# Second sweep of a hybrid encoder layer: the MLA gate product with x as the stationary operand, turned back in 32x32 blocks

## The chip, the cores and the metric

The kernel runs on one core of a Trainium2 chip. The metric is the device time of one execution in microseconds (us), the median of several runs. The profile is of one further execution; its span is counted from the first to the last instruction that the profiler recorded.

The names of the engines follow the profile: PE is TensorE (its weight loads are PEld), DVE is VectorE, ACT is ScalarE, POOL is GpSimd, and SP is the engine whose queue issues nearly all transfers (DMA).

## What is computed

One layer of an encoder over 2048 tokens of width 1024. An input projection of x feeds two groups of heads: a gated linear attention (GLA) and a multi-head latent attention (MLA). The change concerns the gate of the MLA group alone:

```python
h = x @ w_in                      # m_gate: the last 512 columns
...
def mla_branch(c_q, c_kv, k_rope, gate, ...):
    ...
    o = o.transpose(1, 0, 3, 2, 4).reshape(B, S, D_MLA)
    return o * jax.nn.silu(gate)
...
    return jnp.concatenate([o_a, o_b], axis=-1) @ w_out
x = layer_norm(DEEPNORM_ALPHA * x + mixed, ln_g, ln_b)
```

All matrix products of the projections are made from fp32r operands split into a high and a low part: high x high, high x low and low x high are accumulated, so one product over one block of 128 inputs is three matmuls.

## The kernel before, in words

The kernel has four stretches. Sweep A (0 to about 349 us) goes through the 16 chunks of 128 tokens backwards for the GLA. Sweep C, the second sweep (about 349 to 581 us), goes forward in 8 steps of two chunks each. Then come 16 blocks of softmax attention (to about 1110 us), and last the output projection of the 16 chunks with the layer norm, whose first chunks are mixed into the last attention block.

A step of sweep C (`sweep_c`) does for its two chunks j = 0 and 1: the product `ipm` (`c_ip`, matmuls of 448 columns) for the compressed q and kv, the end of the GLA (`Ob`, `c_oib` to `c_oT`), transposes (`tm`), the rotary q (`pqr`), the absorbed q (`pq`) and the MLA gate (`pz`). Each helper `c_...` is one entry with a place, a number in units of a step (tables `PLACE_C`, `PLACE_C_FIRST`, `PLACE_C_LAST`). All entries are sorted by place, and each engine, SP's queue among them, executes its instructions in that order (`in_order`). So a waiting instruction holds up everything behind it on its engine.

The gate before: `c_pz` multiplies 256 tokens at once. The weights are stationary (one 128x128 block for a head h and an input block k), x of both chunks moves, 256 columns wide: 4 heads x 8 blocks x 3 = 96 matmuls a step, in 8 pieces of 12, into a tile `pz` of two PSUM banks, with channels on partitions and tokens along the free axis. Then `c_gm1` to `c_gm3` on ACT (exp, ln(1 + .), exp) and `c_gm4` on DVE make silu of 128x1024 numbers, and `c_sgm` stores them to the scratch tensor `gm_s`. That layout, channels by tokens, is the one the output projection needs.

Buffers that matter here. PSUM tag `gp` has two slots; `Ob`, `pz` and `pq` rotate through them, so `Ob` of the second chunk waits until `gm4` has read `pz`, and the next step's `pz` waits until `c_og` has read that `Ob`. In SBUF the gate tile has tag `gm` with one buffer, and the low part of the absorbed q (`c_qal`) uses the same tag: `gm1` of a step must wait until the store of the previous step's `qal` (`c_sqa`) has landed. The tile `og` (`c_sqO`) has tag `og` with two buffers. `xch` and `xcl`, the split x of the step, have one buffer; `c_xh` and `c_xl` overwrite one chunk's half for the next step.

In the output projection `OutProj.load` issues for a chunk, on SP in this order: four loads of the GLA output `oa_s` (each fills 32 partitions, in runs of 32 numbers, which completes a transpose that DVE made within blocks of 32x32), one load of the gate from `gm_s`, one of the softmax row factors `r_s` and one of the attention output `ob_s`. `gate` on POOL multiplies the attention output by both, `hi` (ACT) and `lo` (POOL) split the result, `part` multiplies. For chunk c the order of work is: split of chunk c+2, load of chunk c+4, product of c, `finish` of c with its stores.

Of the kernel before, what the change touches and what calls it, by code (L numbers as in the profile page):

```python
# [18 lines left out]
P = 128  # L19
S = 2048  # L20
D = 1024
NK = D // P
NCH = S // P
H = 4
# [5 lines left out]
QB = 512  # L30
NQB = S // QB
# [97 lines left out]
    part=(1.05, 2.03, 5.45, 8.05, 10.24, 17.37, 21.96, 27.24),  # L129
# [3 lines left out]


SETUP_C = ("lset", "u15", "u14", "wS", "wH", "wL", "pb0", "wa0", "wh0", "wl0", "pb1", "wa1", "wh1", "wl1")
STEP_C = ("gm1", "gm2", "gm3", "gm4", "sgm", "pq", "qah", "qal", "sqa")
CHUNK_C = ("lx", "xh", "xl", "lS", "lq", "lo", "lu", "sqm", "ssm", "rml", "rmd", "cq", "ckv", "krf", "krfa",
    "krsh", "krsl", "vh", "vl", "kvx", "tm", "cqTh", "cqTl", "ckvTh", "ckvTl", "krT", "pqr", "qrf", "qrfa",
    "tq", "qrTh", "qrTl", "Sf1", "Sf2", "M", "Ob", "oib", "sqO",
    "ss", "rgl", "rgd", "og", "oT", "soT")  # L140

FETCH_C = ("lx", "xh", "xl")
LAST_C = ("ckvTh", "ckvTl", "krT")
# [14 lines left out]
    xh=(-0.19, -0.054),  # L158
    sqO=(0.272, 0.94),
    rgl=(0.283, 1.029),  # L160
# [10 lines left out]
    oT=(0.392, 1.103),  # L171
    oib=(0.24, 0.881),
    ss=(0.278, 1.005),
    rgd=(0.359, 1.067),
# [20 lines left out]
    lx=(-0.578, -0.186),  # L195
    soT=(1.119, 1.45),
    pz=(0.25, 0.306, 0.318, 0.429, 0.527, 0.531, 0.557, 0.559),
    gm1=0.823,
    gm2=0.832,
    gm3=0.837,  # L200
    gm4=0.845,
    sgm=1.17,
    pq=1.435,
    qah=1.501,
# [66 lines left out]
    lx=(-3.463, 0.129),  # L271
    soT=(1.342, 1.45),
    pz=(-0.249, -0.195, -0.111, -0.018, 0.405, 0.452, 0.485, 0.622),
    gm1=0.643,
    gm2=0.815,
    gm3=0.82,
    gm4=0.83,
    sgm=1.056,
    pq=1.431,
    qah=1.57,  # L280
# [50 lines left out]
    lx=(-0.48, -0.573),  # L331
    soT=(1.29, 2.304),
    pz=(0.572, 0.578, 0.707, 0.845, 0.918, 1.023, 1.1, 1.22),
    gm1=1.309,
    gm2=1.608,
    gm3=1.859,
    gm4=1.953,
    sgm=2.042,
    pq=1.525,
    qah=1.948,  # L340
# [13 lines left out]
class K:  # L354
# [151 lines left out]
    def run(self):  # L506
        tc, nc, ins = self.tc, self.nc, self.ins
        with ExitStack() as top:
            cp = top.enter_context(tc.tile_pool(name="const", bufs=1))
            self.cp = cp  # L510
            dp = top.enter_context(tc.tile_pool(name="scr", bufs=1, space=DRAM))
            self.qd_s = [dp.tile([P, H * P], F32, name=f"qd_s{c}") for c in range(NCH)]
            self.oi_s = [dp.tile([P, H * P], F32, name=f"oi_s{c}") for c in range(NCH)]
            self.su_s = [dp.tile([P, H * P], F32, name=f"su_s{c}") for c in range(NCH)]
            self.u_s = [dp.tile([P, H * P], F32, name=f"u_s{c}") for c in range(NCH)]
            self.qa_s = [[dp.tile([P, H, QB], F32, name=f"q{p}_s{b}") for p in "hl"] for b in range(NQB)]
            self.qr_s = [dp.tile([2, QB // P, P, 256], F32, name=f"qr_s{b}") for b in range(NQB)]
            self.gm_s = [dp.tile([P, H, QB], F32, name=f"gm_s{b}") for b in range(NQB)]
            self.kv_s = dp.tile([NCH, 3, P, P], F32, name="kv_s")
            self.oa_s = [dp.tile([H, P, P], F32, name=f"oa_s{c}") for c in range(NCH)]  # L520
            self.qk_s = [[dp.tile([64, H, P], F32, name=f"{n}_s{c}") for c in range(NCH)] for n in ("qx", "kx")]
            self.kt_s = [dp.tile([P, H, P], F32, name=f"kt_s{c}") for c in range(NCH)]
            self.r_s = [dp.tile([1, H, QB], F32, name=f"r_s{b}") for b in range(NQB)]
            self.ob_s = [dp.tile([P, H, QB], F32, name=f"ob_s{b}") for b in range(NQB)]

            ident = cp.tile([P, P], F32, name="ident")
            self.ident = ident
            self.gkv_c = cp.tile([P, 1], F32, name="gkv_c")
            self.gn_c = cp.tile([P, 1], F32, name="gn_c")
# [24 lines left out]
            self.ckvT_h, self.ckvT_l, self.kr = (self.kvT[:, :, i] for i in range(3))  # L554
            self.vh = rp.tile([P, NKT, P], F32R, name="vh")
            self.vl = rp.tile([P, NKT, P], F32R, name="vl")
            self.sweep_c()
            bcs.close()
            psum.close()
            self.wof = top.enter_context(tc.tile_pool(name="wof", bufs=PRE_W, side="right", reuse_waits="tile"))  # L560
            self.attention()
# [693 lines left out]


    def c_pz(self, s, n):
        last = s["st"] == NCH // 2 - 1
        if n == 0:
            s["pz"] = self.gp.tile([P, H, 256], F32, tag="gp", name=f"pz{s['st']}")  # L1260
        order = [(h, k) for h in range(H) for k in range(NK)]
        if last:
            order = [(h, k) for p in range(2) for k in range(NK) for h in (p, p + 2)]
        x2 = lambda t, k: t[:, k].rearrange("p a t -> p (a t)")
        part = [(h, k, p) for h, k in order[4 * n:4 * n + 4] for p in range(3)]
        if n == 0 and s["st"]:

            part.sort(key=lambda e: e[2] == 1)
        stop = {h: (k, p) for h, k, p in part if k == NK - 1}
        for h, k, p in part:  # L1270
            w, x = ((0, self.xch), (0, self.xcl), (1, self.xch))[p]
            self.nc.tensor.matmul(s["pz"][:, h], self.Wz[k][w][:, h * P:(h + 1) * P], x2(x, k),  # L1272
                                  start=(k == 0 and p == 0), stop=stop.get(h) == (k, p))

    def c_gm1(self, s):
        s["gm"] = self.w1.tile([P, H, 256], F32, tag="gm", name=f"gm{s['st']}")
        self.nc.scalar.activation(s["gm"], s["pz"], AF.Exp, scale=-1.0)

    def c_gm2(self, s):
        self.nc.scalar.activation(s["gm"], s["gm"], AF.Ln, bias=1.0)  # L1280

    def c_gm3(self, s):
        self.nc.scalar.activation(s["gm"], s["gm"], AF.Exp, scale=-1.0)

    def c_gm4(self, s):
        self.nc.vector.tensor_tensor(s["gm"], s["pz"], s["gm"], ALU.mult)

    def of_step(self, s):
        return s["st"] // 2, slice((s["st"] % 2) * 256, (s["st"] % 2) * 256 + 256)

    def c_sgm(self, s):
        b, qs = self.of_step(s)
        self.nc.sync.dma_start(self.gm_s[b][:, :, qs], s["gm"])

    def c_pq(self, s):
        pq = s["pq"] = self.gp.tile([P, H, 256], F32, tag="gp", name=f"pq{s['st']}")
# [8 lines left out]
        self.hi(s["qh"], s["pq"])  # L1305

    def c_qal(self, s):
        s["ql"] = self.w1.tile([P, H, 256], F32R, tag="gm", name=f"qal{s['st']}")
        self.lo(s["ql"], s["pq"], s["qh"])

    def c_sqa(self, s):
        b, qs = self.of_step(s)
        for t, dst in zip((s["qh"], s["ql"]), self.qa_s[b]):
            self.nc.sync.dma_start(dst[:, :, qs], t.bitcast(F32))

    def c_sqr(self, s, j):
        b, qs = self.of_step(s)
# [586 lines left out]
class OutProj:  # L1904
# [39 lines left out]
    def load(self, o):  # L1944
# [7 lines left out]
        else:  # L1952
            gr = self.gr[c % 2] = self.gr.get(c % 2) or self.slot(f"gr{c}").rearrange("p a (b d) -> p a b d", b=4)
        o["gr"] = gr
        for r, src in kern.blocks_of(kern.oa_s[c].rearrange("h p (m t) -> h p m t", t=32)):
            nc.sync.dma_start(of[r, 0].rearrange("p h (b t) -> p (h b) t", t=32), src)
        nc.sync.dma_start(gr[:, 0], kern.gm_s[b][:, :, cs])
        nc.sync.dma_start(gr[:, 1], kern.r_s[b][:, :, cs].to_broadcast([P, 4, P]))
        nc.sync.dma_start(of[:, 1], kern.ob_s[b][:, :, cs])
        o["oh"], o["ol"] = [], []  # L1960
# [158 lines left out]
```

## Time and profile before

| | |
|---|---|
| median of 3 runs | 1261.82 us (1261.12 to 1262.24) |
| the profiled execution's own time | 1264.79 us |
| its span | 1262.9 us |
| PE busy | 1239.1 us, 6848 matmuls |
| DVE, ACT, POOL busy | 896.3, 729.1, 726.5 us |
| granted TensorE clock, mean | 0.997 of full speed |
| moved by DMA | 165.59 MB in 277393 packets, 178630 of them under 512 B |

A row of the timeline has the start in us, the duration, the engine, the source line, the operation, its tiles as out<-in and, in brackets, the idle time of the engine before it with what ended it. Matmuls are pipelined: one shows a duration of 0.28 us and more although the next starts 0.12 us later, so the cost of a matmul is read from the distance of starts. Rows of a table of stretches give busy time and instruction count for each engine, then the granted clock, the busy share of the 16 DMA engines and GB/s.

### The profile page before, as it was taken

To read this page: it belongs to the slowest core of one execution; us is meant where nothing else is said; L and a number is where in the kernel's file an instruction comes from. 1 tells how busy PE (TensorE), PEld (TensorE's weight loads), DVE (VectorE), ACT (ScalarE), POOL (GpSimd) and SP (SyncE) were. 2 spreads that over 40 slices of the span, in tenths; PEclk is the share of its full clock that TensorE was granted. 3 is DMA by queue.
4 is the path that set the end of the run, shared out by engine and by line. 5 is a ranking of instruction groups with operands and counts; after the bars stand their busy time and mean duration, and the time that the engine had idled before them with its cause. 6 is when DMAs were issued, how large, how long until landed. Compare 5 with 4: busy or idle time off the path is not lost.

```text
span 1262.9 us, 19554 instructions
## 1 busy us (share of the span) xinstructions
PE 1239.1 (98%) x6848; PEld 1089.6 (86%) x6848; DVE 896.3 (71%) x1666; ACT 729.1 (58%) x1149; POOL 726.5 (58%) x443
## 2 busy tenths in 40 slices
PE   7999999999999999999999999999999999999997
PEld 7999999999899999988788888888888888887886
DVE  6635454554565666665899999999999998378767
ACT  6643434444564444544888888888888888411210
POOL 0132323232355556530798888889999999935551
PEclk9999999999999999999999999999999999999999
DMA  8225555555757788868412222202234110487773
GB/s 294 68 84 130 134 143 139 144 139 144 266 180 212 212 247 244 245 184 210 79 28 49 43 50 43 53 15 59 59 93 93 41 42 26 125 206 212 198 210 100
DMA packets 277393, 165.59 MB, mean 131 GB/s; under 512 B 178630, under 2 KB 234830, under 8 KB 277296
## 3 DMA queue, kind: packets, MB, share of 16 engines
q1 hardware_dynamic: 276176, 162.23, 48.3%
q0 software_dynamic: 672, 2.10, 0.4%
q8 instruction: 54, 0.88, 0.3%
q14 instruction: 43, 0.35, 0.1%
q10 hardware_dynamic: 448, 0.03, 0.0%
HBM read 105.54 MB, written 58.75 MB: 130 GB/s over the span
## 4 chain that ended last, share of the span: by engine, by line
PE 84%; DVE 4%; DMA 4%; POOL 2%; issue 2%; ACT 2%; SPq 1%; DVEq 0%; POOLq 0%; ACTq 0%
PE pz L1272 7%; PE ipm L1341 5%; PE pS L1605 5%; PE pS L1607 4%; PE pS L1606 4%; PE pS L1608 4%; PE pS L1609 4%; PE o L421 4%; PE o L419 4%; PE o L420 4%; PE ipa L419 4%; PE ipa L421 4%; PE ipa L420 4%; PE ipg L421 2%; PE ipg L419 2%
## 5 line engine op out<-in xcount | busy, mean ns | idle before, releaser
L371 POOL TENSOR_TENSOR pl<-s,ph 128x1024 fp32r<-128x1024 f32 x128 | 306.8, 2416 | 47.2 <-ACT ph L365 37.0
L1614 ACT ACTIVATE s<-pS 128x1024 f32<-128x1024 f32 x128 | 131.5, 1028 | 52.9 <-PE pS L1609 49.0
L1627 DVE TENSOR_TENSOR rm<-pS,rm 128x512 f32<-128x512 f32 x210 | 144.6, 689 | 18.3 <-ACT s L1614 12.7
L1651 DVE TENSOR_TENSOR s<-s,mb 128x1024 f32<-128x1024 f32 x128 | 151.2, 1213 | 9.0 <-PE mb L1645 8.9
L365 ACT ACTIVATE ph<-s 128x1024 fp32r<-128x1024 f32 x128 | 134.8, 1056 | 15.7 <-PE o L421 15.1
L1655 ACT ACTIVATE s<-s 128x1024 f32<-128x1024 f32 x128 | 131.6, 1051 | 10.3 <-DVE s L1651 9.6
L419 PE MATMUL ipa<-wah,xah 128*128 128x384 f32 (+1 forms) x384 | 129.2, 336 | 6.1 <-ACT wah L365 6.1
L420 PE MATMUL ipa<-wal,xah 128*128 128x384 f32 (+1 forms) x384 | 125.0, 325 | 0.0
L421 PE MATMUL ipa<-wah,xal 128*128 128x384 f32 (+1 forms) x384 | 124.7, 325 | 0.0
L1091 POOL TENSOR_TENSOR Sb<-Sb,Us 64x512 f32<-64x512 f32 x15 | 19.9, 1327 | 171.5 <-DVE Us L1083 162.3
L1605 PE MATMUL pS<-qh,kvT 128*128 128x512 f32 x256 | 102.6, 401 | 0.8 <-DVE rm L1627 0.4
L419 PE MATMUL o<-ph,vh 128*128 128x512 f32 x256 | 100.9, 394 | 0.0
L1607 PE MATMUL pS<-qh,kvT 128*128 128x512 f32 x256 | 100.0, 391 | 0.0
L1606 PE MATMUL pS<-ql,kvT 128*128 128x512 f32 x256 | 100.0, 390 | 0.0
L421 PE MATMUL o<-ph,vl 128*128 128x512 f32 x256 | 99.8, 390 | 0.0
L1608 PE MATMUL pS<-rh,kvT 128*128 128x512 f32 x256 | 99.8, 390 | 0.0
L1609 PE MATMUL pS<-rl,kvT 128*128 128x512 f32 x256 | 99.8, 390 | 0.0
L420 PE MATMUL o<-pl,vh 128*128 128x512 f32 x256 | 99.7, 389 | 0.0
L1678 DVE TENSOR_TENSOR ap<-ap,s 128x512 f32<-128x512 f32 x120 | 82.9, 691 | 2.7 <-ACT s L1655 0.7
L419 PEld LDWEIGHTS ipa<-wah,xah 128*128 128x128 f32 x384 | 73.3, 191 | 9.3 <-ACT wah L365 6.4
L371 POOL TENSOR_TENSOR ol<-of,oh 128x512 fp32r<-128x512 f32 x32 | 42.5, 1328 | 59.8 <-ACT oh L365 47.4
L1272 PE MATMUL pz<-xch,wzh 128*128 128x256 f32 x256 | 73.4, 290 | 1.4 <-DVE og L1529 1.3
(308 smaller groups left out, 3404.9 us busy)
## 6 DMA issues: line engine op xcount, KB each, us to landing
xcf<-xT_dram SPq DMA_DIRECT2D x16, 512.0 KB, 5.5
xr<-x_dram SPq DMA_DIRECT2D x16, 512.0 KB, 6.0
out_dram<-rr SPq DMA_DIRECT2D x32, 256.0 KB, 3.5
xaf<-xT_dram SPq DMA_DIRECT2D x14, 512.0 KB, 4.2
oib<-oi_s SPq DMA_DIRECT2D x16, 256.0 KB, 4.9
qdb<-qd_s SPq DMA_DIRECT2D x16, 256.0 KB, 3.5
SU<-su_s SPq DMA_DIRECT2D x16, 256.0 KB, 5.0
ub<-u_s SPq DMA_DIRECT2D x16, 256.0 KB, 4.1
```

What stands on the lines that cost most here:

```text
L371: return e.tensor_tensor(dst, src, hi.bitcast(F32), ALU.subtract).ins
L419: mm(out, ah, bh, start=start, stop=False)
L420: mm(out, ah, bl, start=False, stop=False)
L421: mm(out, al, bh, start=False, stop=stop)
L1272: self.nc.tensor.matmul(s["pz"][:, h], self.Wz[k][w][:, h * P:(h + 1) * P], x2(x, k), start=(k == 0 and p == 0), stop=stop.get(h) == (k, p))
L1605: mm(ps[:, e], kh, qh, start=True, stop=False)
L1606: mm(ps[:, e], kh, ql, start=False, stop=False)
L1607: mm(ps[:, e], kl, qh, start=False, stop=False)
L1608: mm(ps[:, e], kr, rh, start=False, stop=False)
L1609: mm(ps[:, e], kr, rl, start=False, stop=True)
L1627: V.tensor_tensor(d["rm"], src[:, e], d["rm"], ALU.max)
L1651: V.tensor_tensor(s, s, d["mb"][:, None, :].to_broadcast([P, 2, QB]), ALU.subtract)
```

## The change

The product is turned round. x of one chunk is stationary, and 512 columns of weights move, so a piece of `pz` is two input blocks of one chunk: 6 matmuls of 512 columns. Pieces 0 to 3 belong to chunk 0, pieces 4 to 7 to chunk 1; their places stay. The result has tokens on partitions. The silu is made for each chunk alone (128x512), its last multiplication is written back into PSUM, and a new entry `gmx` turns it in blocks of 32x32 on DVE into SBUF. The scratch tensor becomes `gm_s[step][chunk, head, 128, 128]`, and the output projection completes the transpose on loading, by four loads with runs of 32 numbers instead of one. The low part of the absorbed q leaves the tag `gm`: it is split into two tiles of tag `og`, made by two instructions and stored by two transfers.

```diff
-STEP_C = ("gm1", "gm2", "gm3", "gm4", "sgm", "pq", "qah", "qal", "sqa")
+STEP_C = ("sgm", "pq", "qah", "qal", "sqa")
@@ CHUNK_C
-    "ss", "rgl", "rgd", "og", "oT", "soT")
+    "ss", "rgl", "rgd", "og", "oT", "soT", "gm1", "gm2", "gm3", "gm4", "gmx")
@@ PLACE_C
-    gm1=0.823,
-    gm2=0.832,
-    gm3=0.837,
-    gm4=0.845,
+    gm1=(0.45, 0.823),
+    gm2=(0.46, 0.826),
+    gm3=(0.47, 0.829),
+    gm4=(0.5, 0.832),
+    gmx=(0.76, 0.835),
...
@@ PLACE_C_FIRST
+    gm1=(0.53, 0.643),
+    gm2=(0.55, 0.815),
+    gm3=(0.56, 0.82),
+    gm4=(0.61, 0.83),
+    gmx=(0.81, 0.835),
...
@@ PLACE_C_LAST
+    gm1=(0.9, 1.309),
+    gm2=(0.91, 1.608),
+    gm3=(1.2, 1.859),
+    gm4=(1.26, 1.953),
+    gmx=(1.265, 1.954),
...
-            self.gm_s = [dp.tile([P, H, QB], F32, name=f"gm_s{b}") for b in range(NQB)]
+            self.gm_s = [dp.tile([2, H, P, P], F32, name=f"gm_s{s}") for s in range(NCH // 2)]
...
     def c_pz(self, s, n):
-            s["pz"] = self.gp.tile([P, H, 256], F32, tag="gp", name=f"pz{s['st']}")
...
+            s["pz"] = self.gp.tile([P, 2, 512], F32, tag="gp", name=f"pz{s['st']}")
+        j, half = divmod(n, 4)
+        for k in (2 * half, 2 * half + 1):
+            xh, xl = self.xch[:, k, j], self.xcl[:, k, j]
+            self.mm3(s["pz"][:, j], xh, xl, self.Wz[k][0], self.Wz[k][1], start=(k == 0), stop=(k == NK - 1))
+
+    def gm(self, d):
+        s, j = d["step"], d["j"]
+        if "gm" not in s:
+            s["gm"] = self.w1.tile([P, 2, 512], F32, tag="gm", name=f"gm{s['st']}")
+        return s["gm"][:, j], s["pz"][:, j]
...
+    def c_gm4(self, d):
+        gm, pz = self.gm(d)
+        self.nc.vector.tensor_tensor(pz, pz, gm, ALU.mult)
+
+    def c_gmx(self, d):
+        self.nc.vector.transpose(*self.gm(d))
...
     def c_sgm(self, s):
-        self.nc.sync.dma_start(self.gm_s[b][:, :, qs], s["gm"])
+        self.nc.sync.dma_start(self.gm_s[s["st"]].rearrange("j h p f -> p (j h) f"),
+                               s["gm"].rearrange("p j (h f) -> p (j h) f", h=H))
...
     def c_qal(self, s):
-        s["ql"] = self.w1.tile([P, H, 256], F32R, tag="gm", name=f"qal{s['st']}")
-        self.lo(s["ql"], s["pq"], s["qh"])
+        s["ql"] = []
+        for n in range(2):
+            hs = slice(2 * n, 2 * n + 2)
+            s["ql"].append(self.w1.tile([P, 2, 256], F32R, tag="og", name=f"qal{s['st']}_{n}", bufs=2))
+            self.lo(s["ql"][n], s["pq"][:, hs], s["qh"][:, hs])
...
     def c_sqa(self, s):
+        qh, ql = self.qa_s[b]
+        self.nc.sync.dma_start(qh[:, :, qs], s["qh"].bitcast(F32))
+        for n, t in enumerate(s["ql"]):
+            self.nc.sync.dma_start(ql[:, 2 * n:2 * n + 2, qs], t.bitcast(F32))
...
@@ OutProj.load
-        for r, src in kern.blocks_of(kern.oa_s[c].rearrange("h p (m t) -> h p m t", t=32)):
-            nc.sync.dma_start(of[r, 0].rearrange("p h (b t) -> p (h b) t", t=32), src)
-        nc.sync.dma_start(gr[:, 0], kern.gm_s[b][:, :, cs])
+        for dst, scr in ((of, kern.oa_s[c]), (gr, kern.gm_s[c // 2][c % 2])):
+            for r, src in kern.blocks_of(scr.rearrange("h p (m t) -> h p m t", t=32)):
+                nc.sync.dma_start(dst[r, 0].rearrange("p h (b t) -> p (h b) t", t=32), src)
```

The functions that the new code calls are unchanged: `blocks_of` yields for m = 0 to 3 the 32 partitions from 32m and the source view, and `mm3` issues high x high, high x low, low x high.

More of the change, by code (lines that the diff above doesn't have):

```diff
@@ L273 @@
     pz=(-0.249, -0.195, -0.111, -0.018, 0.405, 0.452, 0.485, 0.622),
[L274 to L277, printed above, removed]
+    gm1=(0.53, 0.643),
[3 more added lines that the diff above has]
+    gmx=(0.81, 0.835),
     sgm=1.056,
@@ L333 @@
     pz=(0.572, 0.578, 0.707, 0.845, 0.918, 1.023, 1.1, 1.22),
[L334 to L337, printed above, removed]
+    gm1=(0.9, 1.309),
[3 more added lines that the diff above has]
+    gmx=(1.265, 1.954),
     sgm=2.042,
@@ L1257, in c_pz @@
     def c_pz(self, s, n):
-        last = s["st"] == NCH // 2 - 1
         if n == 0:
-            s["pz"] = self.gp.tile([P, H, 256], F32, tag="gp", name=f"pz{s['st']}")
[L1261 to L1286, printed above, removed]
+            s["pz"] = self.gp.tile([P, 2, 512], F32, tag="gp", name=f"pz{s['st']}")
[3 more added lines that the diff above has]
+            self.mm3(s["pz"][:, j], xh, xl, self.Wz[k][0], self.Wz[k][1], start=(k == 0), stop=(k == NK - 1))
@@ new lines, in gm, with c_gm1, c_gm2, c_gm3 @@
+    def gm(self, d):
[3 more added lines that the diff above has]
+        return s["gm"][:, j], s["pz"][:, j]
+    def c_gm1(self, d):
+        gm, pz = self.gm(d)
+        self.nc.scalar.activation(gm, pz, AF.Exp, scale=-1.0)
+    def c_gm2(self, d):
+        gm, _ = self.gm(d)
+        self.nc.scalar.activation(gm, gm, AF.Ln, bias=1.0)
+    def c_gm3(self, d):
+        gm, _ = self.gm(d)
+        self.nc.scalar.activation(gm, gm, AF.Exp, scale=-1.0)
@@ L1288, in of_step @@
+    def c_gm4(self, d):
+        gm, pz = self.gm(d)
+        self.nc.vector.tensor_tensor(pz, pz, gm, ALU.mult)
+    def c_gmx(self, d):
+        self.nc.vector.transpose(*self.gm(d))
     def of_step(self, s):
@@ L1291, in c_sgm @@
     def c_sgm(self, s):
-        b, qs = self.of_step(s)
-        self.nc.sync.dma_start(self.gm_s[b][:, :, qs], s["gm"])
+        self.nc.sync.dma_start(self.gm_s[s["st"]].rearrange("j h p f -> p (j h) f"),
+                               s["gm"].rearrange("p j (h f) -> p (j h) f", h=H))
     def c_pq(self, s):
@@ L1307, in c_qal @@
     def c_qal(self, s):
-        s["ql"] = self.w1.tile([P, H, 256], F32R, tag="gm", name=f"qal{s['st']}")
-        self.lo(s["ql"], s["pq"], s["qh"])
+        s["ql"] = []
[3 more added lines that the diff above has]
+            self.lo(s["ql"][n], s["pq"][:, hs], s["qh"][:, hs])
     def c_sqa(self, s):
         b, qs = self.of_step(s)
-        for t, dst in zip((s["qh"], s["ql"]), self.qa_s[b]):
-            self.nc.sync.dma_start(dst[:, :, qs], t.bitcast(F32))
+        qh, ql = self.qa_s[b]
+        self.nc.sync.dma_start(qh[:, :, qs], s["qh"].bitcast(F32))
+        for n, t in enumerate(s["ql"]):
+            self.nc.sync.dma_start(ql[:, 2 * n:2 * n + 2, qs], t.bitcast(F32))
     def c_sqr(self, s, j):
```

## The prediction

> **What bounds the kernel now.** I read the page first (engines, chain), then the waits, the chain and the timeline of sweep C, and last the stretch in which the output projection starts.
>
> ```profile
> span 1262.9 us, 19554 instructions
> PE 1239.1 (98%) x6848; PEld 1089.6 (86%) x6848; DVE 896.3 (71%) x1666; ACT 729.1 (58%) x1149; POOL 726.5 (58%) x443
> GB/s 294 68 84 130 134 143 139 144 139 144 266 180 212 212 247 244 245 184 210 79 28 49 43 50 43 53 15 59 59 93 93 41 42 26 125 206 212 198 210 100
> DMA  8225555555757788868412222202234110487773
> PE 84%; DVE 4%; DMA 4%; POOL 2%; issue 2%; ACT 2%; SPq 1%; DVEq 0%; POOLq 0%; ACTq 0%
> PE pz L1272 7%; PE ipm L1341 5%; PE pS L1605 5%; PE pS L1607 4%; PE pS L1606 4%; PE pS L1608 4%; PE pS L1609 4%; PE o L421 4%; PE o L419 4%; PE o L420 4%; PE ipa L419 4%; PE ipa L421 4%; PE ipa L420 4%; PE ipg L421 2%; PE ipg L419 2%
> ```
>
> PE is the bound, and the gate product heads the chain by line. A shorter `pz` shortens the run unless PE then waits. DMA is busy in sweep C and once more from 1100 us on; both places count below.
>
> In sweep C steps repeat; these are pieces of the chain of work that ended last (start, duration):
>
> ```profile
> 393.90 2.87 PE pz L1272 x24
> 402.33 0.91 PE Ob L1506 x8
> 411.11 6.07 PE pz L1272 x36
> 425.24 2.87 PE pz L1272 x24
> 440.53 4.31 PE pz L1272 x36
> 452.90 2.87 PE pz L1272 x24
> ```
>
> From 425.24 on the last pieces of a step come every 27.66 us (452.90 - 425.24), with PE busy throughout. From 393.90 to 425.24 it is 31.34 us: 3.68 us are lost once, between step 1 and step 2. The timeline shows where:
>
> ```profile
> 393.15 0.52 SPq L1314 DMA_DIRECT2D ql_s<-qal  x1
> 400.31 1.03 ACT L1277 ACTIVATE gm<-pz 128x1024 f32<-128x1024 f32 x1 [2.46 <-DMA qr_s<-qrT]
> 403.55 1.22 DVE L1286 TENSOR_TENSOR gm<-pz,gm 128x1024 f32<-128x1024 f32 x1 [8.78 <-ACT gm L1283]
> 409.80 0.44 PE L1413 MATMUL tm<-ident,cq 128*128 128x128 f32 x2 [0.83 <-ACT cq L1364]
> 411.11 0.39 PE L1272 MATMUL pz<-xch,wzh 128*128 128x256 f32 x1 [0.88 <-DVE og L1529]
> 410.00:416.00 6.00, 5.12 (x30) 4.89 (x29) 5.84 (x22) 3.16 (x14) 4.91 (x6) 0.72 0.82 227
> ```
>
> `gm1` waits for a store although it reads only PSUM: its buffer is the one that `qal` used, and the store issued at 393.15 is not released before 400.3 (the row names `qr_s`, issued behind it; only `ql_s` holds this buffer). So `gm4` starts at 403.55, the DVE queue behind it is late, `tm` and `pz` wait, and the granted clock falls to 0.72: 36 matmuls take 6.07 instead of 4.31 us.
>
> *The skill on this.* The Trainium skill, "TensorE: Matmul & The Clock Gate", Part 1, lets the clock fall after an idle window of about 3.4 us. By it the two waits would be too short and only some 2 us of the 3.68 would belong to this stall, and the sum below would be -1.8. The trace does not agree: the clock fell after two waits of about 1 us.
>
> **The change, part by part.**
>
> *The matmuls.* Price of 512 columns, from the gate product of sweep A, which has this very form (first and last of 18 matmuls in a row):
>
> ```profile
> 344.73 0.39 PE L419 MATMUL ipg<-wgh,xbh 128*128 128x512 f32 x1
> 348.58 0.39 PE L421 MATMUL ipg<-wgh,xbl 128*128 128x512 f32 x1
> ```
>
> (348.58 - 344.73) / 17 = 0.2265 us. Of 256 columns: 4.31 / 36 = 0.1197. A step goes from 96 x 0.1197 = 11.49 to 48 x 0.2265 = 10.87: 0.62 less, 8 steps: -4.9 us. Twice the columns cost nearly twice the time; this is no halving. In the steady steps PE waits for nothing, so it counts in full; bounds: -5.0, and -4.0 if the first and the last step, whose order waits on DVE, keep theirs. I take -4.8.
>
> *The gate tile unshared.* `gm1` now waits only for its own predecessor's store, a step old. `gm4` of step 1 then follows the end of `pz`, about 3 us earlier. The next thing late would be `og`, whose end at 411.1 lets `pz` start; 3 us earlier it ends before `tm`, which then does not wait either. The stall and the clock loss go: -3.7, between 0 (the wait returns elsewhere, below) and -3.7.
>
> *The silu, turning and splitting.*
>
> ```profile
> L1286 DVE TENSOR_TENSOR gm<-pz,gm x8: 1223/1224/1226, 373.5 to 580.5; 128x1024 f32<-128x1024 f32 x8
> L1563 DVE TENSOR_TENSOR gs<-ipg,gs 128x512 f32<-128x512 f32 x14 | 9.7, 690 | 27.4 <-ACT gs L1561 27.4
> L1535 DVE STREAM_TRANSPOSE oT<-og 128x512 f32<-128x512 f32 x16 | 11.4, 711 | 0.5
> L1557 ACT ACTIVATE gs<-ipg 128x512 f32<-128x512 f32 x14 | 8.4, 598 | 40.3 <-PE ipg L421 38.1 <-DMA k<-kx_s 2.2
> 450.90 1.22 DVE L371 TENSOR_TENSOR qal<-pq,qah 128x1024 fp32r<-128x1024 f32 x1 [1.30 <-ACT qah L365]
> 460.01 1.22 DVE L1286 TENSOR_TENSOR gm<-pz,gm 128x1024 f32<-128x1024 f32 x1 [6.23 <-ACT gm L1283]
> 449.84 1.02 ACT L365 ACTIVATE qah<-pq 128x1024 fp32r<-128x1024 f32 x1 [5.08 <-PE pq L421]
> 455.81 1.06 ACT L365 ACTIVATE xch<-xcf 128x1024 fp32r<-128x1024 f32 x1 [2.28 <-PE pz L1272]
> ```
>
> DVE: one 1.22 becomes 2 x (0.69 + 0.71) = 2.80 a step, and `qal` 1.22 becomes 1.38: +1.7 us. ACT: each 128x1024 becomes two of about 0.6, so +0.5 us. Chunk 0's silu needs `pz` only up to piece 3, which ends before `pq`; three ACT operations (1.9 us) fit in the 5.08 idle before `qah`, `gm4` in the 1.30 before `qal`, `gmx` in the 6.23 after it. Chunk 1's chain after the last piece becomes 3 x 0.6 + 1.4 = 3.2 instead of 4.3, and `xch` of chunk 0 need no longer wait 2.28 for the second half of `pz`. So everything that was tight behind `gm4` (the bank for `Ob`) gets 1 to 3 us of room. Cost on the path: 0; if the cover ahead of `qal` failed, the 0.69 of `gm4` would hold up `qal` and the bank that it frees, 8 times: 5.5.
>
> *SP and stores in sweep C.* One more issue a step (0.52, the row at 393.15), and the gate's store in runs of 512 B instead of 1 KB.
>
> ```profile
> 427.01 0.42 SPq L1318 DMA_DIRECT2D qr_s<-qrT  x1
> 434.60 0.32 SPq L1467 DMA_DIRECT2D qdb<-qd_s  x1
> ```
>
> These two follow each other in SP's queue, so it stands idle for 7 us in a step; 0. The second `og` of a step now waits for the first stored half of `qal`. In step 1 that store was released at 400.3, and `og` comes after `Ob`, which ends at 403.2: some 3 us of room.
>
> *The loads of the output projection.* This is the price. Each chunk trades one load of 512 packets of 512 B for four with 2048 packets of 128 B, three more issues.
>
> ```profile
> 720.00:730.00 10.00, 10.00 (x50) 8.28 (x49) 8.49 (x11) 7.08 (x8) 8.16 (x4) 1.00 0.82 131
> 750.00:760.00 10.00, 10.00 (x49) 8.29 (x48) 8.44 (x12) 7.13 (x8) 8.19 (x5) 1.00 0.62 131
> 1108.00:1128.00 20.00, 20.00 (x92) 16.57 (x91) 14.28 (x29) 2.49 (x7) 7.71 (x6) 1.00 0.92 205
> 1170.00:1230.00 60.00, 60.00 (x267) 49.66 (x266) 42.07 (x71) 9.32 (x23) 34.94 (x24) 1.00 0.73 208
> 1128.30 2.73 SPq L2048 DMA_DIRECT2D out_dram<-rr  x4
> 1135.35 1.29 DVE L2032 SCALAR_TENSOR_TENSOR rr<-xr,po 128x512 f32<-128x512 f32 x2 [1.78 <-DMA out_dram<-rr]
> 1139.59 0.63 ACT L365 ACTIVATE oh<-of 128x512 fp32r<-128x512 f32 x1
> 1147.03 0.50 PE L421 MATMUL pmb<-woh,ol 128*128 128x512 f32 x1 [1.00 <-POOL ol L371]
> 1218.39 1.92 SPq L1956 DMA_DIRECT2D of<-oa_s  x4
> 1234.19 2.98 POOL L1965 TENSOR_TENSOR of<-of,gr 128x512 f32<-128x512 f32 x2
> ```
>
> The first two rows hold one query fetch of attention each: 4096 packets of 128 B and 384 of 2 KB. 0.62 x 10 us x 16 engines = 99 engine-us. At 23 GB/s an engine (294 / (0.8 x 16), first slice) the 384 take 34, which leaves 16 ns a small packet; all on the small ones is 24, the busier fetch (131) at most 32. I take 20. The load then costs 2048 x 0.020 - 512 x 0.022 = 30 engine-us more, 1.9 us of all 16 engines a chunk (1.4 to 3.4).
>
> Three such loads, of chunks 4 to 6, are issued in the 20 us before the stores at 1128.30, where DMA is 0.92 busy and leaves 1.6 us free. Behind them in SP's queue stand the x loads and the stores at 1128.30, whose landing frees the buffer for the residual at 1135.35; `finish`, in front of chunk 6's split on ACT (1139.59), follows it, and PE already waits for that split at 1147.03. There is no slack, so 3 x 1.9 = 5.6, less 1.6, arrives on PE: 4.0 to 5.6, and 0.5 for the later wait behind the next x load: +5.0 (1.0 if only the issues count, 3 x 0.48 less the room; more in the second rival).
>
> Later it is hidden: chunk 15's load starts at 1218.39 and the gate takes it at 1234.19. Of these 15.8 us some 4 go to the issues and up to 7 to the landing (the slow store at 393.15); the 5 left cover the 1.9 and three issues of 0.48 (1.92 / 4). 127 of 174 engine-us a chunk (0.73 x 16 x 10.9 us) become 157.
>
> *The skill on this.* The Trainium skill, "DMA: Bandwidth & Descriptors", Specifications, asks for at least 512 B a transfer and says that smaller ones are read, modified and written. As an estimate, 128 B would then cost no less than 512 B, 22 ns, the load 34 engine-us, and the tail about 0.8 us more than by the 20 that the fetch shows: -2.7 for the sum below, inside the forecast's own range.
>
> *Sum.* -4.8 - 3.7 + 5.0 = -3.5. The profiled execution, 1264.79 (span 1262.9 and 1.9 around it), becomes 1261.3; the median lies 2.97 below that execution, so 1258.3.
>
> **The rivals.**
>
> *The tail absorbs the loads.* If small packets cost 16 ns and the 0.08 free share takes most of it, PE loses 1.0: -7.5, 1254.3. For it: from 1170 on a quarter of DMA is free. Against: the chain through 1135.35 has no room.
>
> *The tail chokes (slower).* One mechanism: the queue of 128 B packets between 1107 and 1140. At 32 ns a chunk costs 3.4 us more; four chunks (4 to 7) 13.6, less 2.7 free: 10.9, and the wait of PE at chunk 6 becomes long enough for the clock, 1.8 as at 411.11: 12.7 in place of 5.0, so +4.2, 1266.0. It decides from (174 - 127 + 11) / 2048 = 28 ns, where the steady chunks fill DMA too. For it: the busier fetch. Against: most fetches show 0.62.
>
> *The stall only moves.* `og`, waiting for `qal`'s store, keeps ACT's queue late in step 1: -4.8 + 5.0 = +0.2, 1262.0. For it: DMA is saturated there, and a store took 7 us. Against: the 3 us of room computed above.
>
> **How the numbers follow.** Forecast 0.42 (own range 1256.3 to 1260.3, the tail between 3 and 7), absorbed 0.20, choked 0.20, moved 0.18. A measurement can tell 0.2%, 2.5 us, from no change: faster is below 1259.3, slower above 1264.3 or, for a case near zero with its own scatter, a part of it. Faster: two thirds of the forecast (0.28) and absorbed (0.20), 0.48. Same: a third of the forecast (0.14) and two thirds of moved (0.12), 0.26. Slower: choked (0.20) and the rest of moved (0.06), 0.26. The range reaches below the absorbed case, where its 1.0 can vanish, and to the choked one: 1253.0 to 1266.0.
>
> **What would show it.** Starts of `pz` matmuls 0.2265 apart and steps of about 27.0 us; no DMA wait ahead of `gm1`, step 1 to 2 as long as the others, clock 1.00 at 410; DMA share above 0.95 between 1108 and 1140, PE's wait for chunk 6 about 4 us longer, no new wait after 1170. I am wrong if `pz` starts waiting for `gm4` or `gmx`, or if chunks after 7 wait for their loads.

## The result, and the profile after

| | before | after |
|---|---|---|
| median of six runs, us | 1261.6 (1260.62 to 1262.24) | 1272.28 (1269.66 to 1273.28) |
| ratio, 95% interval | | 1.0082 (1.0069 to 1.0095) |
| the profiled execution, its span | 1264.79, 1262.9 | 1272.72, 1271.0 |

The changed kernel is 10.7 us slower. The prediction said 1258.3, with 1253.0 to 1266.0 as the range.

The page of the changed kernel (span, engines, DMA packets, and engines along the chain that ended last):

```profile
span 1271.0 us, 18931 instructions
PE 1239.7 (98%) x6464; PEld 1070.6 (84%) x6464; DVE 909.3 (72%) x1698; ACT 733.3 (58%) x1173; POOL 726.0 (57%) x443
DMA packets 306960, 165.56 MB, mean 130 GB/s; under 512 B 212294, under 2 KB 264398, under 8 KB 306864
PE 81%; issue 5%; DMA 4%; POOL 3%; DVE 3%; SPq 2%; ACT 2%; DVEq 0%; POOLq 0%; ACTq 0%
```

384 matmuls fewer, and PE is as busy as before: 1239.7 against 1239.1. A busy PE includes matmuls at a lower clock, so the shorter product must have been paid for somewhere. PE's share of the chain fell from 84 to 81%. The list of what PE waited for (total, times, longest) names the places:

```profile
PE ipa L422 <- ACT wah L368: 5.5, 1, 5.5
PE pmb L422 <- DVE rr L2043: 3.5, 3, 1.7
PE pz L422 <- DVE rg_t L446: 2.9, 1, 2.9
PE pqr L424 <- DVE cqT_l L374: 2.2, 1, 2.2
```

The first is the start of the kernel, which the change does not touch. `pmb` (the output projection) waiting for `rr`, and `pz` (the new product) waiting for L446, are new. First the stall that was to go, the same stretch as in the prediction:

```profile
410.00:416.00 6.00, 6.00 (x35) 5.23 (x34) 5.81 (x23) 3.39 (x13) 2.64 (x4) 1.00 0.92 245
```

The clock is 1.00 where it was 0.72: the stall between step 1 and step 2 is gone. But step 0 has a new one. The chain through it, piece by piece (start, duration):

```profile
365.78 0.60 ACT gm L1276
...
366.65 0.53 ACT gm L1280
...
367.20 0.64 ACT gm L1284
...
367.86 0.10 DVE pz L1288
367.96 0.51 issue
368.47 0.16 DVE rg_t L446
368.63 0.78 PE pz L422
369.41 0.43 PE pz L423
369.83 0.43 PE pz L424
```

PE stops after piece 3 and starts piece 4 only when `gm4` of chunk 0 (L1288, issued 367.86, 0.70 long) has ended at 368.56. The chain names `rg_t`, the next instruction on DVE, since it ended nearest; the dependence is on `gm4`. Piece 4 writes `pz[:, 1]`, `gm4` writes `pz[:, 0]`; they share no number, but they are one tile. And after the wait the clock is half: 0.43 us a matmul instead of 0.23, and a granted clock of 0.50 from 369.41 to 371.50.

In the steady steps the same dependence leaves a gap (`gm4` of chunk 0, the last row of `pq` and the first rows of piece 4, then one whole step as a stretch):

```profile
447.22 0.67 DVE L1288 TENSOR_TENSOR pz<-pz,gm 128x512 f32<-128x512 f32 x1
447.65 0.28 PE L424 MATMUL pq<-cqT_h,wabs_l 128*128 128x256 f32 x1
447.94 0.50 PE L422 MATMUL pz<-wzh,xch 128*128 128x512 f32 x1
448.28 0.40 PE L423 MATMUL pz<-wzl,xch 128*128 128x512 f32 x1
```

```profile
426.48:453.93 27.45, 27.44 (x154) 24.49 (x153) 19.42 (x66) 14.44 (x39) 15.13 (x17) 1.00 0.84 240
```

0.29 instead of 0.12 us behind `pq`, 0.34 instead of 0.23 behind the first matmul: a step takes 27.45, not 27.0. In the last step a mere reading does the same: `gm1` of chunk 0 stands right ahead of piece 4 there (places 0.9 and 0.918), and piece 4 waits until `gm1` has read its half:

```profile
570.28 0.60 ACT L1276 ACTIVATE gm<-pz 128x512 f32<-128x512 f32 x1 [1.78 <-PE pz L424]
570.93 0.50 PE L422 MATMUL pz<-wzh,xch 128*128 128x512 f32 x1 [0.69 <-ACT gm L1276]
```

In all sweep C gained nothing and took 1.8 us more: the first score product of attention (`pS`) starts at 580.48, before at 580.50, although the changed execution had entered sweep C 1.8 us earlier (first `ipm` of the sweep at 346.99 against 348.81).

The rest is lost in the output projection. SP's queue, DVE and PE around chunk 4, then the stretches ahead of and behind the stall, after and (counted from the same product, `sx`) before:

```profile
1109.93 2.47 SPq L1968 DMA_DIRECT2D gr<-gm_s  x4
...
1113.60 1.05 SPq L1989 DMA_DIRECT2D xr<-x_dram  x2
...
1121.03 0.27 PE L1758 MATMUL rt<-ident,rc 128*4 128x128 f32 x1 [0.78 <-DVE rc L1746]
...
1122.22 0.69 DVE L2043 SCALAR_TENSOR_TENSOR rr<-xr,pmb 128x512 f32<-128x512 f32 x1 [1.03 <-DMA xr<-x_dram]
...
1123.05 0.77 PE L422 MATMUL pmb<-woh,oh 128*128 128x512 f32 x1 [1.75 <-DVE rr L2043]
...
1133.26 2.54 SPq L2059 DMA_DIRECT2D out_dram<-rr  x4
```

```profile
1107.65:1119.65 12.00, 12.00 (x54) 9.88 (x53) 6.91 (x14) 0.63 (x1) 2.09 (x2) 1.00 0.90 216
1119.65:1129.65 10.00, 7.47 (x29) 5.78 (x28) 8.27 (x19) 1.85 (x6) 4.30 (x4) 0.83 0.64 125
```
```profile
1107.75:1119.75 12.00, 12.00 (x55) 9.88 (x53) 7.77 (x16) 0.63 (x1) 3.46 (x3) 1.00 0.99 229
1119.75:1129.75 10.00, 10.00 (x48) 8.34 (x47) 8.51 (x18) 1.85 (x6) 5.92 (x5) 1.00 0.80 163
```

`pmb` of chunk 4 needs a PSUM bank, which chunk 2's residual (`rr<-xr,pmb`) frees, which waits for its x load, issued at 1113.60 behind the four gate loads. The stores stand in SP's queue 4.96 us later than before (1133.26 against 1128.30). The DMA engines are not what became the limit: their share is 0.90 and then 0.64, in the kernel before 0.99 and 0.80. From the start of attention to chunk 15's product it is 671.25 us (580.48 to 1251.73), before 663.24 (580.50 to 1243.74): 8.0 more.

### The profile page after: what moved, and what is told of

It is laid out like the page before. It is cut to its first block, busy times and chain, and to the rows that moved or that the text cites. A ratio compares the mean times of both kernels' runs of the same rounds, so it can differ in the third digit from the quotient of the medians.

```text
span 1271.0 us, 18931 instructions
## 1 busy us (share of the span) xinstructions
PE 1239.7 (98%) x6464; PEld 1070.6 (84%) x6464; DVE 909.3 (72%) x1698; ACT 733.3 (58%) x1173; POOL 726.0 (57%) x443
## 4 chain that ended last, share of the span: by engine, by line
PE 81%; issue 5%; DMA 4%; POOL 3%; DVE 3%; SPq 2%; ACT 2%; DVEq 0%; POOLq 0%; ACTq 0%
PE ipm L1352 5%; PE o L422 5%; PE o L423 5%; PE o L424 5%; PE pS L1616 4%; PE pS L1618 4%; PE pS L1617 4%; PE pS L1620 4%; PE pS L1619 4%; PE ipa L422 4%; PE ipa L424 4%; PE ipa L423 4%; PE pz L422 2%; PE pz L424 2%; PE pz L423 2%
## 5 line engine op out<-in xcount | busy, mean ns | idle before, releaser
L423 PEld LDWEIGHTS ipa<-wal,xah 128*128 128x128 f32 x384 | 73.0, 190 | 0.8 <-DVE wal L374 0.3
```

Of the source, the lines that this page charges most:

```text
L423: mm(out, ah, bl, start=False, stop=False)
```

## The experiments

Each ratio is to the kernel before, with its 95% interval. The theories after the comparison: the tail pays for the loads (for their packets, or for their number); sweep C pays for the one tile `pz`; or sweep C's end eats any lead.

**The unshared tile alone.** The kernel before, with the `qal` and `sqa` of the change:

```diff
-        s["ql"] = self.w1.tile([P, H, 256], F32R, tag="gm", ...)
+            s["ql"].append(self.w1.tile([P, 2, 256], F32R, tag="og", ..., bufs=2))
```

> The kernel before with one part of the change alone: the low part of the absorbed q in two tiles of tag og, stored by two transfers; product, silu, scratch layout and output projection as before. Both theories expect the stall between step 1 and step 2 (3.68 us) to go, so that the steps from step 2 on start about 3.7 us earlier than before. Theory A (a lead that sweep C gains is kept): attention starts 3.7 us earlier, 1261.6 - 3.7 = 1257.9. Theory B (the last step of sweep C waits for loads that come no earlier, and eats any lead): attention starts at 580.5 as before, 1261.6.

Measured: 1259.26 (0.9987, 0.9978 to 0.9995), 2.5 less. The stretch between step 1 and step 2 is a normal step now:

```profile
394.58:422.24 27.66, 27.66 (x202) 26.97 (x201) 17.90 (x63) 13.85 (x36) 15.13 (x16) 1.00 0.82 242
```

Attention starts at 574.80, 5.7 earlier: 2.0 of this it had already when sweep C began (346.78), 3.7 is the stall. The lead is kept; theory B falls. That the median gained 2.5 and not 3.7 fits the scatter that the last run below shows.

**One gate load; four gate loads with long runs.** The changed kernel with other loads in the output projection:

```diff
-        for dst, scr in ((of, kern.oa_s[c]), (gr, kern.gm_s[c // 2][c % 2])):
...
+        nc.sync.dma_start(gr[:, 0], kern.gm_s[c // 2][c % 2].rearrange("h p f -> p h f"))
```
```diff
+        for m in range(4):
+            r = slice(32 * m, 32 * m + 32)
+            nc.sync.dma_start(gr[r, 0], kern.gm_s[c // 2][c % 2][:, r].rearrange("h p f -> p h f"))
```

> The changed kernel with one gate load per chunk in the output projection again, 512 packets of 512 B; the transpose of the gate that the four loads complete is left out, so the gate factors stand in the wrong places. Theory A (the four loads with 128 B runs cost the tail its 8.0 us): the product of chunk 4 starts at about 1120.1 instead of 1123.05, chunk 15 some 8 us earlier, 1272.3 - 8 = 1264.3. Theory B (the tail lost time to something else that came with the change, the order of its instructions or the clock): less than 3 us back, over 1269.

> The changed kernel with four gate loads per chunk, each of 32 partitions in runs of 512 B: three more issues than the kernel before, its number and size of packets; the transpose of the gate is left out. Theory A (the packets cost): as with one load, about 1264.3. Theory B (the three issues on SP cost, 3 x 0.48 us a chunk ahead of the x loads): most of the 8 us stays, 1269 to 1272.

Measured: 1261.43 (0.9999, 0.9989 to 1.0008) and 1267.14 (1.0049, 1.0034 to 1.0065). So the loads cost 10.8 us, by the medians the whole loss: 5.7 for three more issues a chunk (each of 32 partitions instead of one of 128), 5.1 for runs of 128 instead of 512 B. Neither theory had it alone. How the time gets to PE is seen at chunk 6: the issue of its x load on SP, and its residual on DVE, whose end frees the bank for chunk 8. Before, one load, four long, and the changed kernel:

```profile
1158.56 0.62 SPq L1978 DMA_DIRECT2D xr<-x_dram  x1
1165.21 0.69 DVE L2032 SCALAR_TENSOR_TENSOR rr<-xr,pmb 128x512 f32<-128x512 f32 x1 [5.49 <-DMA xr<-x_dram]
```
```profile
1156.01 0.61 SPq L1989 DMA_DIRECT2D xr<-x_dram  x1
1162.67 0.69 DVE L2043 SCALAR_TENSOR_TENSOR rr<-xr,pmb 128x512 f32<-128x512 f32 x1 [4.87 <-DMA xr<-x_dram]
```
```profile
1159.96 0.62 SPq L1991 DMA_DIRECT2D xr<-x_dram  x1
1166.24 0.69 DVE L2045 SCALAR_TENSOR_TENSOR rr<-xr,pmb 128x512 f32<-128x512 f32 x1 [7.31 <-DMA xr<-x_dram]
```
```profile
1165.93 0.62 SPq L1989 DMA_DIRECT2D xr<-x_dram  x1
1172.24 0.69 DVE L2043 SCALAR_TENSOR_TENSOR rr<-xr,pmb 128x512 f32<-128x512 f32 x1 [7.55 <-DMA xr<-x_dram]
```

In all four the residual follows the issue by 6.3 to 6.7 us. By these rows the load takes no longer with small packets around it; it is issued later. Counted from `sx` (a product for the softmax sums of the last head; 1119.75, 1118.84, 1118.51, 1119.65), the issue comes after 38.8, 37.2, 41.5 and 46.3 us. Part of that is SP's own time for the issues: the gate loads of chunks 4 to 6 take 6.1 us of the queue before (1.44, 3.68 and 0.97) and 9.9 after (2.47, 5.06 and 2.41). Part is a loop that the changed kernel's chain shows from 1109 on (a load's landing, the split on ACT and POOL that frees a buffer, SP's next loads, their landing):

```profile
1109.33 3.68 DMA of<-oa_s
1113.03 0.64 ACT oh L368
1113.74 1.30 POOL ol L374
...
1116.19 2.18 SPq L1968
1118.42 6.01 DMA of<-oa_s
```

The Trainium skill, "Perfetto Trace Analysis", What "DMA-bound" means, tells two main cases apart: the 16 engines, or the sequencer that issues, whose track is then solid. The trace agrees that this is the second: from chunk 4's load to the first stores (1107.90 to 1133.26) the changed kernel's SP has no gap of 0.2 us and waits for a semaphore in 4.8 of the 25.4 us, while the DMA share is 0.64 to 0.90. What made one issue last 2.18 us there, where others take 0.49, stays open.

**The order of the instructions.** With four loads the compiler had also moved two things of the last heads forward: `rt`, which turns softmax row factors, ahead of chunk 4's product on PE, and `rc`, which computes such factors, ahead of chunk 2's residual on DVE. Put back, with four long loads:

```diff
+                            with self.in_order({ENGINES[2]: rest[2]["aggr"]}, ENGINES[2:3]):
+                                f(nb - 1)
...
+                        with self.in_order({ENGINES[0]: pe5}, ENGINES[:1]):
                             turn(nb - 2)
```

> The four gate loads of 512 B runs once more (transpose of the gate left out), with the instructions of TensorE and VectorE in the order of the kernel with one load: rt of the last head but one goes back behind the product of chunk 5, and the sum rc of the last head behind the aggregate of chunk 2. Both had moved forward when the loads became four. Theory A (the three issues on SP, in front of the x loads, cost the 5.7 us between one load and four): 1267. Theory B (the order that the compiler chose costs it: rt and rc stand ahead of pmb): 1261 to 1262.

Measured: 1266.67 (1.0038, 1.0024 to 1.0051). The order costs nothing that can be told from scatter (0.5); the 5.7 stay with the three issues.

**The loads alone, in the kernel before.** Its gate load made into four by tokens, 128 B runs:

```diff
-        nc.sync.dma_start(gr[:, 0], kern.gm_s[b][:, :, cs])
+        for m in range(4):
+            t = slice(32 * m, 32 * m + 32)
+            nc.sync.dma_start(gr[:, 0, :, t], kern.gm_s[b][:, :, cs][:, :, t])
```

> The kernel before with its gate load split into four by tokens, each in runs of 32 numbers: 2048 packets of 128 B and three issues more per chunk, everything else as before, sweep C included. Theory A (the loads alone cost what the tail of the changed kernel lost, 5.1 for packets and 5.7 for issues by the two runs with wide loads): 1261.7 + 10.8 = 1272.5. Theory B (part of that loss belongs to the later or slower arrival from sweep C): 1265 to 1269.

Measured: 1275.77 (1.0109, 1.0089 to 1.013), 14.5 more. Without the change such loads alone cost more than its whole loss, and more than expected. They are not quite the same loads: each of these fills all 128 partitions, each of the change 32. What makes the difference to 10.8 stays open. In the profiled execution, 4.4 over the median of its kernel, PE's waits at chunk 6 and 8 (2.45 and 2.78 us) cost clock as well, which is 0.91 over 40 us there.

**The silu of chunk 0 behind the last piece.** The changed kernel with other places, here for the middle steps:

```diff
-    gm1=(0.45, 0.823), gm2=(0.46, 0.826), gm3=(0.47, 0.829), gm4=(0.5, 0.832), gmx=(0.76, 0.835),
+    gm1=(0.822, 0.823), gm2=(0.825, 0.826), gm3=(0.828, 0.829), gm4=(0.831, 0.832), gmx=(0.834, 0.835),
```

and, in a second kernel, with `gm1` to `gm3` of chunk 0 left at 0.45 to 0.47 in the middle steps.

> The changed kernel with the silu of chunk 0 and its turning moved behind the last piece of pz, right ahead of those of chunk 1. Theory A (pieces 4 to 7, which write the other half of pz, wait for the silu of chunk 0 because the whole tile is tracked): the wait of 2.9 us in step 0 and the gap ahead of piece 4 in each step go, steps of about 27.2 instead of 27.46 us, the product of step 1 starts 2 to 3 us earlier; in the end 1268 if the lead is kept, 1272 if the last step eats it. Theory B (the wait has another cause, the DVE queue): nothing changes in step 0, and the longer chain behind the last piece, 6 x 0.63 + 4 x 0.71 = 6.6 us instead of 3.2, holds the bank that Ob needs: 1273 to 1280.

> The changed kernel with only gm4 and gmx of chunk 0 behind the last piece of pz; its exp, ln and exp stay where the change put them in the middle steps (in the first and the last step all are behind it, as in the earlier run). If only the write of gm4 into pz holds up piece 4, steps are 27.2 us as there and the chain behind the last piece is shorter by 3 x 0.63: 1264 to 1266. If the reading by gm1 of chunk 0 holds up piece 4 as well: steps of 27.4 to 28 us, 1267 or more.

Measured: 1265.77 (1.0037, 1.0022 to 1.0051) and 1265.39 (1.003, 1.0017 to 1.0042), 6.5 and 6.9 less than the changed kernel. A step of the first:

```profile
449.21:476.38 27.17, 27.17 (x154) 24.43 (x152) 19.21 (x66) 13.87 (x39) 15.18 (x17) 1.00 0.82 240
```

Starts of the first chunk's `ipm`, us:

| | sweep C | after step 1 | last step | `pS` |
|---|---|---|---|---|
| changed kernel | 346.99 | 398.86 | 536.14 | 580.48 |
| silu behind the last piece | 346.93 | 394.76 | 530.71 | 574.32 |
| unshared tile alone | 346.78 | 394.58 | 532.88 | 574.80 |

The wait of PE for one half of a tile cost 4.0 us in steps 0 and 1, 0.27 in each of five steps, and 0.7 in the last. In the middle steps it is the write of `gm4` that holds piece 4: with `gm1` to `gm3` early a step takes 27.17 as well. There `gm1` has read its half some 2 us before piece 4 comes; where it stands right ahead of piece 4, in the last step of the changed kernel, the reading holds it too (0.69, the rows at 570). In step 1 both kernels have a wait of 0.92 for `og`, which neither the changed kernel nor the unshared tile alone has, and they gain nothing over the latter in steps 0 and 1; that the longer chain behind the last piece makes this wait is not shown.

**The x loads of chunks 2 and 3 ahead of chunk 4's loads,** added to the second of these:

```diff
-                load(4)
                 for c in (2, 3):
                     op.load_res(rest[c])
+                load(4)
```

> As the run before it, and the x loads of chunks 2 and 3 issued ahead of chunk 4's loads instead of behind them. Theory A (the tail is slow because the x loads stand behind the gate loads on SP, and the residual of chunk 2, which frees the bank that chunk 4's product needs, waits for them): no wait of PE for DVE rr at chunk 4, 2 to 4 us less than the run before it, 1261 to 1263. Theory B (the tail waits for bandwidth, whatever is first): the wait moves to the split of chunks 4 to 6, 1264 to 1267.

Measured: 1267.25 (1.0042, 1.0027 to 1.0058), 1.9 more. PE's wait of 0.63 for `rr` at chunk 4 is gone. The waits for the splits of chunk 6 are 3.2 us (1.83, 0.66 and 0.73) instead of 2.3, and a new one of 1.2 for the split of chunk 4 has come. Moving one load ahead in a full queue moved the wait.

**The gate loads on ACT's queue,** same base: `nc.scalar.dma_start` for the four loads.

> The kernel with gm4 and gmx of chunk 0 behind the last piece (1265.4), its four gate loads per chunk with 128 B runs now issued from ACT's queue instead of SP's; number and size of packets unchanged. Theory A (on SP the three extra issues hold up the x loads and stores behind them, 5.7 us): 1265.4 - 5.7 = 1259.7. Theory B (a load costs wherever it is issued, or ACT now holds up the split that PE waits for): 1264 to 1270.

Measured: 1262.42 (1.0005, 0.9995 to 1.0014), 3.0 less than on SP, not 5.7: an answer between the two theories. It is no clean division. The four issues now hold up ACT for 1.9 to 2.4 us a chunk (rows of 1.93, 1.98 and 2.38 between its splits), PE still waits 1.06 and 1.00 us for the split of chunk 6, and the compiler moved `sx` behind the product of chunk 5 (1137.28, in the run on SP 1112.06). The DMA engines are busy at 0.98 and 0.97 there (1106 to 1118 and to 1128), so they may be what limits this kernel. What each of these costs stays open. This run gives the price of a packet, as the gate loads have ACT's queue to themselves (page, DMA queues; before, this queue had 448 packets and 0.0%):

```profile
q10 hardware_dynamic: 34240, 4.23, 2.3%
```

2.3% of 16 engines over 1261.8 us are 464 us, for 33792 packets more, 32768 of them (16 x 2048) the runs of 128 B: about 14 ns each.

**All of it but the loads and the wait.** One load of long runs on the same base:

> The same kernel with one gate load of 512 B runs per chunk (the transpose of the gate is left out): the change without its loads and without the wait for gm4. If the three parts add up (5.1 for packets, 5.7 for issues, some 6.9 for the wait): 1265.4 - 10.8 = 1254.6, about 6.7 under the kernel before, against the 8.5 that the prediction gave to sweep C. If the tail only waits for something else: 1258 or more.

Measured: 1255.22 (0.9944, 0.9931 to 0.9956). The parts add up.

**The second half of the turn moved to the stores.** The silu of chunk 0 behind the last piece, one load as above, and in sweep C eight stores a step of 128 B runs instead of one, at place 1.59 (2.042 in the last step), where SP has nothing to issue:

```diff
+        for j in range(2):
+            dst = self.gm_s[s["st"]][j].rearrange("h (m a) f -> a (h m) f", a=32)
+            for b in range(4):
+                t = slice(32 * b, 32 * b + 32)
+                self.nc.sync.dma_start(dst[:, :, t], s["gm"][t, j].rearrange("a (q t) -> a q t", t=32))
```

> The second half of the transpose moved from the loads of the output projection to the stores of sweep C: eight stores a step with 128 B runs, issued in a gap of 3.4 us on SP (behind the loads of SU and oib), and one load of 512 B runs per chunk; the silu of chunk 0 behind the last piece, as in the earlier run (1265.8). Everything is computed. Theory A (SP and DMA have room in sweep C that they lack in the output projection; 8 issues of 0.5 us in the gap, DMA share 0.84 there plus 0.08 for the packets): the tail as with one load, 1265.8 - 10.5 = 1255.3, under both kernels. Theory B (the stores delay the loads behind them, qdb and xcf): each of the six middle steps 0.5 to 1.5 us longer, 1258 to 1265.

Measured: 1255.73 (0.995, 0.9932 to 0.9969). As many small packets as in the changed kernel and one issue a step more, 6.4 us under the kernel before and 16.5 under the changed one: in sweep C SP has the room. The stretch from step 1 to step 2 takes 28.11 instead of 27.28, but then a step takes 27.17 as before. The x load of chunk 6 goes out 36.0 us after `sx`, earlier than in the four kernels compared above:

```profile
1152.99 0.62 SPq L1992 DMA_DIRECT2D xr<-x_dram  x1
```

**The kernel before, once more,** unchanged, for a second profile.

> The kernel before, unchanged, for a second profile of it. The first one starts sweep C at 348.81 and loses 3.68 us between step 1 and step 2; it took 1264.79, 3.0 over the median. If start and stall scatter from execution to execution, the unshared tile is worth less on average than the 3.7 of that one profile: start at 347 to 348, a stall of 1 to 3 us, 1261 to 1262. If the profile was typical: start at 349, stall 3.7, and the 2.5 us that the run with the tile alone gained are scatter of the medians.

Measured: one run, 1259.06. The stretch from step 1 to step 2, and from the timeline what `gm1` waits for:

```profile
394.32:423.27 28.95, 28.07 (x202) 27.02 (x201) 17.25 (x62) 13.73 (x36) 15.13 (x16) 1.00 0.80 235
```
```profile
397.12 1.03 ACT L1277 ACTIVATE gm<-pz 128x1024 f32<-128x1024 f32 x1 [1.54 <-DMA ql_s<-qal]
```

The stall is 28.95 - 27.66 = 1.29 us here, and the clock stays 1.00. In the kernel before with small loads the same step took 32.05 (397.51 to 429.56), a stall of 4.39. So it scatters between 1.3 and 4.4 in three executions, and the 2.5 that the median lost by it lies between. The start of sweep C scatters too: 346.52 here, 348.81 in the first profile.

## Why the prediction was wrong, point by point

*The account.* By medians: unshared tile -2.5 (1259.26 - 1261.75); product, silu and turn without their wait and with the old kind of load -4.0 (1255.22 - 1259.26); the wait for the silu of the other half +6.7 (mean of 6.5 and 6.9); the loads +10.5 (mean of 10.8 and 10.2). Sum +10.7, measured +10.7: wait and loads cost the same, to 0.7 us, whichever is taken away first. The prediction had -3.7, -4.8, 0 and +5.0.

*What bounds the kernel.* Right: each loss that was traced came to the end time as a wait or a lost clock of PE.

*The matmuls, -4.8.* Right in kind, too large in size. With the wait taken away a step takes 27.17 instead of 27.66, 0.49 and not 0.62 less, because matmuls of 512 columns start 0.2294 apart here (434.62 to 438.29 for 16, in the kernel with `gm4` late), not the 0.2265 of sweep A: 48 x 0.2294 = 11.0 instead of 11.49. And only five steps gain it. That kernel's steps 0 and 1 and its last one are as long as with the unshared tile alone (47.85 against 47.80, 41.88 against 41.92). So sweep C gained 2.4, outside the stated bounds of -5.0 to -4.0. The medians of the account give 4.0; the other 1.6 have no part of the product to show for them. In the two profiles 1.9 lie between `pS` and chunk 15's product (661.83 against 663.75), and their cause stays open.

*The gate tile, -3.7.* The mechanism was right: the rows at 410 show it, and `og` did not wait for `qal`'s store, so the rival that the stall only moves fell. The price was that of one execution, in which two waits happened to cost the clock; by the medians it was worth 2.5.

*The silu: "Cost on the path: 0".* This step failed. The prediction asked which other work hides the DVE and ACT time, and did not ask who else writes the tile that `gm1` now reads and `gm4` now writes. What the runs showed in its place is +6.7: piece 4 waits for the silu of the other half. Its last paragraph named the sign (`pz` waiting for `gm4`) without a price. The case that it did price, `gm4` holding up `qal`, did not come.

*SP and stores in sweep C, 0.* Right: the unshared tile alone, with the extra store, has steps of 27.66; even eight stores more fit.

*The loads, +5.0.* This step failed most, and in its reading of the resource; measured are 10.5. It counted engine time of packets (20 ns; measured about 14) against the free share of 16 DMA engines, and gave the issues alone 1.0, three of 0.48 once. But SP was the full one: in the kernel before the queue had no gap of 0.2 us from 1107.08 to 1131.03, with 3.9 us of semaphore waits in it, so three issues of 0.5 us at each of three loads, 4.5 as an estimate, arrive behind it. Measured, the issues cost 5.7, and the packets 5.1 more. That they do so by landing later inside the loop of loads and buffers is an inference from the chain, not shown by a run. The path was another one too: the prediction followed the stores to PE's wait for chunk 6, and that grew by 0.7 only (from 0.29 and 1.00 to 0.96 and 1.01), while PE came to wait for residuals that wait for x loads, 1.75 at chunk 4 and 1.49 at chunk 8. "Later it is hidden" fell as well: the first stores were 5.0 us late, chunk 6's x load 7.4 (1165.93 against 1158.56), and PE waited once more ahead of chunk 8's product, at 1173.

*The rivals.* The choked tail had the sign and nearly the place, but not the cause: its sign was a DMA share above 0.95, and the share went down (0.90 and 0.64). The absorbed tail fell.

*The Trainium skill on small transfers.* The Trainium skill, "DMA: Bandwidth & Descriptors", Specifications, was read in the prediction as 22 ns for 128 B. The trace does not agree with that price (about 14 ns). It agrees with the advice to stay at 512 B, since four loads of long runs are 5.1 us faster than four of short ones.

## What to carry to other kernels

Count a transfer first as an issue on the queue that makes it: here that queue had no gap, and three more issues of 0.5 us a chunk ahead of loads that PE needs cost 5.7 us in all, while the DMA share of the same stretch went from 0.90 to 0.86. When operations are moved to read and write a tile in parts while another engine still fills the rest, look at the tile, not at the part: here one half held up the other, and other places for the silu of chunk 0 were worth 6.7 us. A price read from one execution of a wait that hangs on a transfer is one draw; a second profile of the kernel before would have shown 1.3 beside 3.7.

## What the runs showed of the hardware

The clock falls, or not, after the same waits. At the end of sweep C the two kernels with a late `gm4` have nearly the same waits of PE; stretches of the first kernel (all of chunk 0's silu late), then of the second:

```profile
547.47 0.39 PE L424 MATMUL pqr<-wqr_h,cqT_l 128*128 128x256 f32 x1 [1.47 <-DVE cqT_l L374]
550.06 1.11 PE L1352 MATMUL ipm<-wmh,xcl 128*128 128x448 f32 x2 [1.03 <-POOL xcl L374]
```
```profile
548.00:554.00 6.00, 4.96 (x23) 4.48 (x23) 4.84 (x20) 0.86 (x3) 3.01 (x3) 0.60 0.59 190
```
```profile
547.40 0.39 PE L424 MATMUL pqr<-wqr_h,cqT_l 128*128 128x256 f32 x1 [1.49 <-DVE cqT_l L374]
549.99 0.67 PE L1352 MATMUL ipm<-wmh,xcl 128*128 128x448 f32 x2 [1.03 <-POOL xcl L374]
```
```profile
548.00:554.00 6.00, 4.97 (x39) 4.53 (x38) 5.43 (x20) 1.11 (x3) 2.96 (x3) 1.00 0.53 180
```

1.47 and 1.03 us of waiting gave a clock of 0.60, 1.49 and 1.03 gave 1.00. From there to `pS` it is 24.26 and 22.51 us, so the draw is worth 1.75 us. The Trainium skill, "TensorE: Matmul & The Clock Gate", Part 1, says that the clock follows a window of about 3.4 us that runs free of the kernel; that fits such a draw, though no run here shows the window itself. In the prediction the same section was set aside for its 3.4 us of idle time; what it says of the window's phase was not used, and it would have warned that the clock's share of the 3.68 us was no fixed price.

And the number of loads changed the order that the compiler gave PE and DVE in the output projection. In the kernel with four long loads it was harmless (0.5 us), in the others it was not tried; a comparison of two kernels has to look at it.
